# A hybrid decoder block on one core: shift columns by matmul, scaling on another engine, HGRN keys and states in other steps, first maxima under more matmuls

## The chip, the cores and the metric

The kernel runs on one core of a Trainium2 chip. The metric is the device time of one execution, in microseconds (us); the figure given for a kernel is the median of its runs. TensorE (PE in the profile, PEld for its weight loads) multiplies and writes to PSUM, VectorE (DVE) and ScalarE (ACT) read and write SBUF and PSUM, GpSimd (POOL) works on SBUF alone, and SyncE (SP) issues most DMAs. Each engine works through its own queue in order and waits at the head of it for whatever the next instruction needs.

## The reference, cut to what matters

The block has 2048 positions of width 1024. Everything is float32.

```python
mod = c_act @ w_ada + b_ada                       # shift, scale, gate, twice
h = rms_norm(x, norm1_g) * (1 + scale1) + shift1
hq, hf, hi, hgt, aq, ak, av = split(h @ w_in)
hg = hgrn2(hq, hf, hi, hgt)       # gated linear recurrence, 4 heads of 128, chunkwise
att = dilated_attention(aq, ak, av)  # 8 heads of 64, three (window, dilation) branches
x = x + gate1 * (concat(hg, rms_norm(att)) @ w_out)
h = rms_norm(x, norm2_g) * (1 + scale2) + shift2
x = x + gate2 * ((silu(h @ Wg) * (h @ Wu)) @ w_down)
out = rms_norm(x, final_g)
```

In the recurrence the state of a chunk is the decayed state before it plus keys times values, and a position's output is the query against the state before its chunk plus the scores inside the chunk times the values.

## The kernel before, in words

A float32 product is made of three fast matmuls: both operands are split into a high part and the rest (hi and lo), and hi·hi, hi·lo and lo·hi are added up in PSUM. A 512-wide matmul of this kind is called a **big** one below.

**Front.** `c_act` is known early. For each of the 8 blocks k of 128 features, `ada_sums` loads two 128x1024 blocks of `w_ada` (shift and scale; tile `adaw`, four buffers), DVE multiplies and adds them by k (two chains of 128x256 in `adaacc`, L105 and L107), and PE adds over the partitions with four matmuls against a column of ones (L110). A matmul with one output column is called a **small** one. ACT makes the shift (`mods`, L496) and scale (`gs1`, L497). `h_apply` then makes block k of the modulated input of the first chunk of 512 positions: times `rstd_x`, scaled and shifted on ACT (L416), split into `hhi` (ACT, L417) and `hlo`. The first and last of these steps run on POOL for chunk 0 and on DVE for the others. `token_major_k` (L463 to L465) multiplies block k with the weights of the values, twelve big matmuls a block. POOL also makes the low parts of the weights (`wlo`, in `split_w`). PE's order is written out by hand: small matmuls of block k, then the twelve big ones of block k-1.

**The two halves.** `first_half` and `second_half` run the input projection for two chunks each: `hg_project` and `att_qk` by `feature_major` (L565 to L567), `token_major` for the values. After every third big matmul `tick` runs the class `Beside`, which puts one step of other work between the matmuls when enough of them have passed: `begin(work, matmuls, steps)` spreads the steps over that many matmuls. The work is `hg_mix`, a generator that yields between steps. There are 16 units of it (4 heads, 4 chunks), two to a `begin`, and 33 steps are reckoned for the two. A unit makes gates and decays, transposes the decayed keys `kd` on PE (L620) to `kt` (copied by ACT, L622), makes `u` = keys times values (L657) and from it the states `hst` (DVE, L664 and L666), then the scores of seven levels (L677): PE writes a level's scores to the PSUM tile `psL`, DVE copies them under a mask into `hsc` (L680 or L682), and `level` prepares the products `hz` of the level two further on (POOL `hd`, ACT exp L644, DVE `hz`). The output `psO` (L693, L694) takes the states and `hsc`, and is normalised.

PSUM has eight banks here: four `psA` for the projections, two `psM`, one `psL`, one `psO`.

**The passage to attention.** After `second_half` the pool of the recurrence is closed, `open_attention` loads queries and keys of head 0, and `maxima(0)` runs its 24 steps between the last 96 big matmuls (`att_qk(1, 3)`), the first of them after 36. Then `combine(0)` joins the maxima of the three branches through DRAM (`m_d`, `mr`, `mn_d`), and the heads follow one after another; the maxima of head 1 (tile `psS`) come first there. SP issues all of these loads and the stores of `att_qk` from one queue.

The order of DVE, ACT, POOL and SP is made by a scheduler when the kernel is built; that of PE in these stages is that of the program.

Of the kernel before, what the change touches and what calls it, by code (L numbers as in the profile page):

```python
# [11 lines left out]
F32 = mybir.dt.float32  # L12
# [4 lines left out]
ALU = mybir.AluOpType  # L17
# [3 lines left out]
P = 128  # L21
# [9 lines left out]
CH = 512  # L31
NCH = S // CH
# [18 lines left out]
def hybrid_block(ctx, tc, xT, small, cst, w_ada, w_ft, w_tk, w_out, w_gu, w_dn, out):  # L51
# [27 lines left out]
    def tt(eng, o, a, b, op):  # L79
        return eng.tensor_tensor(o, a, b, op)  # L80
# [12 lines left out]
        act.activation(dst, dst, AF.Exp, scale=-0.5)  # L93


    def ada_sums(pl, cact, gs, bufs, psum, chains=1):

        w = pl.tile([P, 2, 8, P], F32, name="adaw", tag="adaw", bufs=bufs)
        acc = [pl.tile([P, 2, P], F32, name="adaacc", tag="adaacc", bufs=2 * chains) for _ in range(chains)]
        for j, g in enumerate(gs):  # L100
            nc.sync.dma_start(out=w[:, j].rearrange("p k c -> p (k c)"), in_=w_ada[g])
        for k in range(8):
            a = acc[k % chains]
            if k < chains:
                dve.tensor_scalar(a, w[:, :, k, :], cact[:, k:k + 1], None, ALU.mult)  # L105
            else:
                dve.scalar_tensor_tensor(a, w[:, :, k, :], cact[:, k:k + 1], a, ALU.mult, ALU.add)  # L107
        ps = psum()
        for j, a in [(j, a) for j in range(2) for a in range(chains)]:
            pe.matmul(ps[:, j:j + 1], acc[a][:, j, :], ones[:, 0:1], start=j + a == 0, stop=j + a == chains,  # L110
                      skip_group_check=True)
        return ps

    m_d = [[dram.tile([S], F32, name=f"m_d{h}_{n}") for n in range(2)] for h in range(8)]
# [223 lines left out]
    with ExitStack() as ab:  # L338
# [70 lines left out]

        def h_apply(c, k, t=None):  # L410
            hhi, hlo = h_of[c]
            eng = pool if c == 0 else dve
            if t is None:
                t = xs1[k] if c == 1 else load_xk(c, k)
            tt(eng, t, t, rstd_x[c], ALU.mult)
            act.activation(t, t, AF.Identity, scale=gs1[:, k:k + 1], bias=sh1[:, k:k + 1])  # L416
            act.copy(hhi[:, k, :], t)  # L417
            return tt(eng, hlo[:, k, :], t, hhi[:, k, :].bitcast(F32), ALU.subtract).ins

        def make_h(c):  # L420
            if c > 1:
# [46 lines left out]
        with tc.tile_pool(name="ada0", bufs=2) as pl:  # L468
            xs0 = []
            for k in range(KT):  # L470
                xs0.append(pl.tile([P, CH], F32, name=f"x0_{k}", bufs=1))
                nc.sync.dma_start(out=xs0[k], in_=xT[:, k, 0:CH])
            x_stats(0, xs0)
            h_tiles(0)
            ps0 = [pp.tile([P, CH], F32, name="psA", tag="psA", bufs=4) for _ in range(4)]
            tags = itertools.cycle(("psM", "psL"))

            def psum():
                tag = next(tags)
                return pp.tile([P, CH], F32, name=tag, tag=tag, bufs=2 if tag == "psM" else 1)  # L480

            LAG0 = 1

            bg = pl.tile([P, 8], F32, name="bg", bufs=1)
            dve.scalar_tensor_tensor(bg, sm[:, V_B + 8:V_B + 16], 1.0, sm[:, V_G1:V_G1 + 8], ALU.add, ALU.mult)
            sums, ws0 = {}, {}
            with tc.manual_schedule(engines={mybir.EngineType.PE}):
              done = {}
              for k in range(KT + LAG0):
                  if k < KT:  # L490
                      sums[k] = ada_sums(pl, cact, (k, 8 + k), 4, psum, 2)
                      if k % 2 == 0:
                          ws0[k] = ws0[k + 1] = split_w(wp, w_tk[0, k // 2])
                  if 0 < k <= KT:
                      n = k - 1
                      act.activation(mods[:, n:k], sums[n][:, 0:1], AF.Identity, bias=sm[:, V_B + n:V_B + k])  # L496
                      act.activation(gs1[:, n:k], sums[n][:, 1:2], AF.Identity, scale=sm[:, V_G1 + n:V_G1 + k],  # L497
                                     bias=bg[:, n:k])
                      with tc.issue_after(done[n - 2]) if n > 1 else nullcontext():
                          done[n] = h_apply(0, n, xs0[n])  # L500
# [92 lines left out]
        def hg_mix(hd, c, x):  # L593
# [21 lines left out]
            yield  # L615
            yield
            yield
            kt_ps = pp.tile([P, CH], F32, name="psM", tag="psM", bufs=2)
            for n in range(4):
                pe.transpose(kt_ps[:, n * P:(n + 1) * P], kd[:, n * P:(n + 1) * P], ident)  # L620
            kt = T("hkt")
            act.copy(kt, kt_ps)  # L622

            sc = T("hsc")
            lr = T("hd", 2)
# [20 lines left out]
                tt(dve, w(z)[:, :, 1, :], w(dd)[:, :, 1, :], w(q)[:, :, 1, :], ALU.mult)  # L646

            level(1)
            yield

            v = v_of[c]
            vn = [v[:, n, hd * P:(hd + 1) * P] for n in range(4)]
            ns = range(3 if c == NCH - 1 else 4)
            u = pp.tile([P, CH], F32, name="psM", tag="psM", bufs=2)
            for n in ns:
                ts = slice(n * P, (n + 1) * P)
                pe.matmul(u[:, ts], kt[:, ts], vn[n], start=n == 0, stop=n == ns[-1], skip_group_check=True)  # L657
            before = [states[hd]]
            for n in ns:
                ts = slice(n * P, (n + 1) * P)  # L660
                new = hw.tile([P, P], F32, name="hst", tag=f"hst{hd}", bufs=2) if n == 3 else \
                    hw.tile([P, P], F32, name="hst", tag="hst", bufs=3)
                if before[-1] is None:
                    dve.tensor_copy(new, u[:, ts])  # L664
                else:
                    dve.scalar_tensor_tensor(new, before[-1], eb[:, n * P + 127:n * P + 128], u[:, ts],  # L666
                                             ALU.mult, ALU.add)
                before.append(new)
            if len(ns) == 4:
                states[hd] = before[4]  # L670
# [40 lines left out]
        def units(hd, xs):  # L711
            return [hg_mix(hd, c, x) for c, x in xs.items()]
# [54 lines left out]

        first_psum = []

        def first_maxima():  # L770

            tags = itertools.cycle(("psL", "psO", "psM", "psM"))

            def psum():
                tag = next(tags)
                return pp.tile([P, CH], F32, name=tag, tag=tag, bufs=2 if tag == "psM" else 1)
            first_psum.append(psum)
# [631 lines left out]
```

## Time and profile before

| | us |
|---|---|
| time, median of 3 runs (lowest, highest) | 3009.27 (3007.25, 3016.14) |
| time of the profiled execution | 3006.01 |
| its span, first to last instruction | 3004.2 |
| PE busy | 2829.4 (94%) |
| DVE, ACT, POOL busy | 2041.7, 1313.2, 1404.8 |
| front, until the last product of chunk 0 | 0 to 68.9 |
| first and second half with the recurrence | 68.9 to about 908 |
| passage to attention | about 908 to 964 |

A row of the timeline gives start, busy time, engine, line, operation, tiles written and read, and a count; in brackets stands the idle time of the engine just ahead of it and what ended it. PE's matmuls overlap, so that the step from one start to the next is what a matmul takes. Mean granted clock of TensorE: 0.979 of full speed.

### The profile page before, as it was taken

What the parts mean: (1) busy time and instruction counts of PE and PEld (TensorE: products, weight loads), DVE (VectorE), ACT (ScalarE), POOL (GpSimd) and SP (SyncE); (2) the same over time, 40 slices, a digit from 0 to 9 for tenths busy, and PEclk for the clock granted to TensorE, in tenths of its full rate; (3) what the DMA queues carried; (4) which work ended last, traced back from release to release, by engine and by line L of the source; (5) the groups of instructions that cost most, each with busy time, mean ns of one, the idle gap of its engine ahead of it and who ended that gap; (6) DMA issues with size and microseconds to landing.
All of it is one profiled execution on the core that took longest, in us unless ns stands there. A gap on an engine that the chain in (4) does not pass through costs nothing. (4 is left out here: it accounts for less than half of the span.)

```text
span 3004.2 us, 45023 instructions
## 1 busy us (share of the span) xinstructions
PE 2829.4 (94%) x16308; PEld 2601.9 (87%) x16308; DVE 2041.7 (68%) x3781; ACT 1313.2 (44%) x2392; POOL 1404.8 (47%) x1076
## 2 busy tenths in 40 slices
PE   6899999999997999999999999999999998999998
PEld 4777777787776999997778999999999998999998
DVE  7677756355554565677777676688677669776676
ACT  4533445344331665666554333345333335443334
POOL 5333443434332232320045666557566655665664
PEclk9999999999997999999999999999999999999999
DMA  6422335111138474537843222123242222232221
GB/s 245 151 99 103 111 141 180 62 64 69 55 116 210 120 164 104 134 109 251 294 158 130 82 73 85 64 78 108 83 133 74 81 71 93 85 114 65 84 75 66
DMA packets 212319, 344.37 MB, mean 115 GB/s; under 512 B 24816, under 2 KB 97392, under 8 KB 209008
## 3 DMA queue, kind: packets, MB, share of 16 engines
q1 hardware_dynamic: 202272, 323.40, 34.9%
q10 hardware_dynamic: 9824, 18.09, 1.6%
q8 instruction: 128, 2.10, 0.3%
q14 instruction: 95, 0.78, 0.1%
HBM read 282.44 MB, written 58.98 MB: 114 GB/s over the span
## 5 line engine op out<-in xcount | busy, mean ns | idle before, releaser
L80 POOL TENSOR_TENSOR wlo<-wraw,whi 128x512 fp32r<-128x512 f32 (+1 forms) x542 | 850.0, 1589 | 480.5 <-ACT whi L87 222.1
L1003 PE MATMUL psG<-chi,whi 128*128 128x344 f32 (+1 forms) x1848 | 596.4, 323 | 20.8 <-DVE hm L80 14.1
L1005 PE MATMUL psG<-chi,wlo 128*128 128x344 f32 (+1 forms) x1848 | 591.9, 320 | 1.5 <-POOL wlo L80 1.5
L1004 PE MATMUL psG<-clo,whi 128*128 128x344 f32 (+1 forms) x1848 | 593.2, 321 | 0.0
L274 ACT CAST whi<-wraw 128x512 fp32r<-128x512 f32 x520 | 311.0, 618 | 403.9 <-issue 191.6
L1003 PEld LDWEIGHTS psG<-chi,whi 128*128 128x128 f32 x1848 | 350.3, 190 | 26.5 <-DVE hm L80 9.3
L1265 PE MATMUL psD<-ahi,whi 128*128 128x344 f32 (+1 forms) x1056 | 346.5, 328 | 20.2 <-DVE xc L1268 19.7
L1268 DVE SCALAR_TENSOR_TENSOR xc<-psD,mods,xc 128x344 f32<-128x344 f32 (+1 forms) x528 | 290.2, 568 | 91.8 <-PE psD L1267 91.5
L1005 PEld LDWEIGHTS psG<-chi,wlo 128*128 128x128 f32 x1848 | 349.3, 189 | 2.7 <-POOL wlo L80 2.7
L1004 PEld LDWEIGHTS psG<-clo,whi 128*128 128x128 f32 x1848 | 349.1, 189 | 0.3 <-issue 0.2
L80 POOL TENSOR_TENSOR wlo<-wt,whi 128x512 fp32r<-128x512 f32 x132 | 192.6, 1469 | 314.6 <-ACT whi L274 238.3
L1267 PE MATMUL psD<-ahi,wlo 128*128 128x344 f32 (+1 forms) x1056 | 338.0, 320 | 0.0
L1266 PE MATMUL psD<-alo,whi 128*128 128x344 f32 (+1 forms) x1056 | 337.0, 319 | 0.0
L80 DVE TENSOR_TENSOR hm<-hm,psG 128x344 f32<-128x344 f32 (+1 forms) x330 | 165.8, 502 | 236.9 <-PE psG L1005 236.5
L565 PE MATMUL psA<-hhi,whi 128*128 128x512 f32 x640 | 272.1, 425 | 4.3 <-ACT hhi L417 2.6
L567 PE MATMUL psA<-hhi,wlo 128*128 128x512 f32 x640 | 253.9, 397 | 0.0
L566 PE MATMUL psA<-hlo,whi 128*128 128x512 f32 x640 | 253.0, 395 | 0.6 <-DVE hlo L80 0.6
L1265 PEld LDWEIGHTS psD<-ahi,whi 128*128 128x128 f32 x1056 | 199.4, 189 | 36.1 <-DVE xc L1268 31.7
L80 POOL TENSOR_TENSOR hd<-hb 128x256 f32<-128x256 f32 x192 | 130.7, 704 | 155.4 <-DVE hz L80 123.3
L1266 PEld LDWEIGHTS psD<-alo,whi 128*128 128x128 f32 x1056 | 199.6, 189 | 0.5
L1267 PEld LDWEIGHTS psD<-ahi,wlo 128*128 128x128 f32 x1056 | 199.5, 189 | 0.0
L274 ACT CAST whi<-wt 128x512 fp32r<-128x512 f32 x132 | 81.4, 616 | 235.0 <-DVE wt L80 139.4
(244 smaller groups left out, 5996.6 us busy)
## 6 DMA issues: line engine op xcount, KB each, us to landing
wraw<-in_w_gu SPq DMA_DIRECT2D x264, 256.0 KB, 2.9
wraw<-in_w_dn SPq DMA_DIRECT2D x132, 256.0 KB, 2.9
adaw<-in_w_ada SPq DMA_DIRECT2D x48, 512.0 KB, 4.8
wraw<-in_w_ft SPq DMA_DIRECT2D x42, 512.0 KB, 3.5
wraw<-in_w_tk SPq DMA_DIRECT2D x32, 512.0 KB, 3.5
qk_d<-st SPq DMA_DIRECT2D x64, 256.0 KB, 2.3
v<-v_d SPq DMA_DIRECT2D x16, 1024.0 KB, 6.1
wraw<-in_w_out SPq DMA_DIRECT2D x64, 256.0 KB, 3.6
```

The lines of the kernel that those rows point to most:

```text
L80: return eng.tensor_tensor(o, a, b, op)
L274: copy(hi, raw)
L565: pe.matmul(ps, whi[:, ws], hhi[:, k, :], start=k == 0, stop=False)
L566: pe.matmul(ps, whi[:, ws], hlo[:, k, :], start=False, stop=False)
L567: pe.matmul(ps, wlo[:, ws], hhi[:, k, :], start=False, stop=k == 7)
L1003: pe.matmul(ps, w[0][:, ws], hi, start=start and k == 0, stop=False, skip_group_check=True)
L1004: pe.matmul(ps, w[0][:, ws], lo, start=False, stop=False, skip_group_check=True)
L1005: last = pe.matmul(ps, w[1][:, ws], hi, start=False, stop=stop and k == 3, skip_group_check=True)
L1265: pe.matmul(ps, w[z][0][:, ws], ahi, start=z == 0, stop=False)
L1266: pe.matmul(ps, w[z][0][:, ws], alo, start=False, stop=False)
L1267: pe.matmul(ps, w[z][1][:, ws], ahi, start=False, stop=z == 1)
L1268: dve.scalar_tensor_tensor(x, ps, ga2[:, j:j + 1], x, ALU.mult, ALU.add)
```

## The change

Four things are changed.

- `ada_sums` becomes `ada_column`. The shift column of block k is now made by eight small matmuls straight from the weights, and only the scale column goes through DVE's chains, which are 128 instead of 256 wide; two small matmuls add them up. `psL` has two buffers here as `psM` has.
- `h_apply` runs its two POOL steps on DVE for chunk 0 too, and no longer waits for the block before the last.
- In `hg_mix` the transposes of the keys (`turn`) come behind the first level's scores and the state updates behind the third level's, each in a step of its own (15 yields where there were 14). `psL` has two banks, and the output `psO` takes one of the two in turn; the bank of its own is gone.
- 48 big matmuls (`att_qk(1, 2)` on the last chunk) go from the last `begin` of the recurrence, whose 33 steps are now spread over 144 and not 192, behind `first_maxima`. The maxima are spread over 62 matmuls, the first after 50 and no longer 36, and `combine(0)` is a step of the same list, so that it stands between the big matmuls.

```diff
-    def ada_sums(pl, cact, gs, bufs, psum, chains=1):
+    def ada_column(pl, cact, k, bufs, psum):
...
+        acc = [pl.tile([P, P], F32, name="adaacc", tag="adaacc", bufs=4) for _ in range(2)]
+        for j, g in ((1, 8 + k), (0, k)):
...
+                dve.scalar_tensor_tensor(a, w[:, 1, k, :], cact[:, k:k + 1], a, ALU.mult, ALU.add)
         ps = psum()
-        for j, a in [(j, a) for j in range(2) for a in range(chains)]:
-            pe.matmul(ps[:, j:j + 1], acc[a][:, j, :], ones[:, 0:1], start=j + a == 0, stop=j + a == chains,
+        for k in range(8):
+            pe.matmul(ps[:, 0:1], w[:, 0, k, :], cact[:, k:k + 1], start=k == 0, stop=False, skip_group_check=True)
+        for a in range(2):
+            pe.matmul(ps[:, 1:2], acc[a], ones[:, 0:1], start=False, stop=a == 1, skip_group_check=True)
...
-            eng = pool if c == 0 else dve
...
-            kt_ps = pp.tile([P, CH], F32, name="psM", tag="psM", bufs=2)
...
             for lv in range(7):
+                if lv == 1:
+                    yield
+                    kt = turn()
+                elif lv == 3:
+                    yield
+                    before = state_updates(kt)
                 yield
                 zk, zq = zs.pop(lv)
-                ps = pp.tile([P, CH], F32, name="psL", tag="psL", bufs=1)
+                ps = pp.tile([P, CH], F32, name="psL", tag="psL", bufs=2)
...
-            o_ps = pp.tile([P, CH], F32, name="psO", tag="psO", bufs=1)
+            o_ps = pp.tile([P, CH], F32, name="psO", tag="psL", bufs=2)
...
-            beside.begin(units(3, xs), 192, 2 * UNIT + 1)
+            beside.begin(units(3, xs), 144, 2 * UNIT + 1)
             att_qk(1, 1)
-            att_qk(1, 2)
+            att_qk(1, 2, (2,))
...
-            beside.begin([maxima(0, psum)], 96 - 36, 24, -36)
+            beside.begin([maxima(0, psum), iter((combine(0, psum) for _ in range(1)))], 62, 24, -50)
...
+            att_qk(1, 2, (3,))
             att_qk(1, 3)
             beside.finish()
-        combine(0, first_psum[0])
```

How the order of the engines moves, at three places. The first is PE at the start, from the sum over squares (`ssq`) on. Before:

```order
L402 MATMUL psM<-ssq,ones 128x512
L110 MATMUL psM<-ones,adaacc 128x1 x4
L110 MATMUL psL<-ones,adaacc 128x1 x4
L463 MATMUL psA<-whi,hhi 128x512
L464 MATMUL psA<-wlo,hhi 128x512
L465 MATMUL psA<-whi,hlo 128x512
```

And in the changed kernel:

```order
L404 MATMUL psM<-ssq,ones 128x512
L111 MATMUL psM<-cact,adaw 128x1 x8
L113 MATMUL psM<-ones,adaacc 128x1 x2
L111 MATMUL psL<-cact,adaw 128x1 x8
L113 MATMUL psL<-ones,adaacc 128x1 x2
L464 MATMUL psA<-whi,hhi 128x512
L465 MATMUL psA<-wlo,hhi 128x512
L466 MATMUL psA<-whi,hlo 128x512
```

Ten small matmuls stand in a block's place where four stood, eight of them reading the weights as they were loaded.

The second place is ACT in the third unit of the recurrence, around the copy of the turned keys (`hkt`). `he` are the exponentials of a unit's gates, 128x1536, and `hd` at L644 (L638 in the changed kernel) the decays of a level. Before:

```order
L598 ACTIVATE he<-he 128x1536
L644 ACTIVATE hd<-hd 128x512 x2
L519 CAST st<-psA 128x512
L87 CAST whi<-wraw 128x1024
L644 ACTIVATE hd<-hd 128x512
L599 ACTIVATE he<-he 128x1536
L606 ACTIVATE hlf<-hfv 128x512
L622 COPY hkt<-psM 128x512
```

And in the changed kernel:

```order
L598 ACTIVATE he<-he 128x1536
L638 ACTIVATE hd<-hd 128x512 x2
L605 ACTIVATE hlf<-hfv 128x512
L638 ACTIVATE hd<-hd 128x512
L651 COPY hkt<-psM 128x512
L638 ACTIVATE hd<-hd 128x512
L87 CAST whi<-wraw 128x1024
```

The copy comes one level further on, behind `hlf` and one more `hd`. On PE 9 big matmuls stood between the transposes and `u` in this unit; now 21 big ones and the scores of two levels do.

The third place is SP at the end of the maxima of head 0: `qk_d<-st` are stores of `att_qk`, `m_d` and `mr` the maxima on their way, `kh` a load for head 1. Before:

```order
L575 DMA qk_d_0_86<-st 128x512
L150 DMA m_d_1_130<-mc 128x16
L153 DMA mr<-m_d_0_129 16x128
L576 DMA qk_d_1_87<-st 128x512
L213 DMA kh<-qk_d_0_80 64x2048
L153 DMA mr<-m_d_1_130 16x128
```

And in the changed kernel:

```order
L155 DMA mr<-m_d_0_129 16x128
L152 DMA m_d_1_130<-mc 128x16
L215 DMA kh<-qk_d_0_80 64x2048
L155 DMA mr<-m_d_1_130 16x128
L574 DMA qk_d_0_78<-st 128x512
L575 DMA qk_d_1_79<-st 128x512
```

The last four stores of `att_qk` come behind the load of `kh` and no longer ahead of it. On PE 30 big matmuls follow the last maxima of head 0, where none did; ahead of the first maxima stand 57 behind the last unit's sum of squares, where 54 stood.

## Rows read from the trace of the kernel before

**Rows 1.** Groups (--lines), 15 to 66 us, on DVE and POOL: busy, mean ns, idle.

```profile
L107 DVE SCALAR_TENSOR_TENSOR adaacc<-adaw,cact,adaacc 128x256 f32<-128x256 f32 x48 | 35.1, 796 | 0.0
L105 DVE TENSOR_SCALAR adaacc<-adaw,cact 128x256 f32<-128x256 f32 x16 | 9.6, 640 | 4.3 <-PE psM L110 1.9 <-DMA adaw<-in_w_ada 1.6 <-PE psL L110 0.9
...
L80 POOL TENSOR_TENSOR hlo<-x,hhi 128x512 fp32r<-128x512 f32 x8 | 14.7, 1833 | 11.2 <-ACT hhi L417 11.2
L80 POOL TENSOR_TENSOR wlo<-wraw,whi 128x1024 fp32r<-128x1024 f32 x5 | 12.5, 2496 | 0.0
L80 POOL TENSOR_TENSOR x<-x,rstd 128x512 f32<-128x512 f32 x8 | 11.0, 1377 | 16.7 <-ACT rstd L93 16.7
```

**Rows 2.** Timeline, DVE in the front, two runs of instructions with POOL idle.

```profile
27.30 2.45 DVE L107 SCALAR_TENSOR_TENSOR adaacc<-adaw,cact,adaacc 128x256 f32<-128x256 f32 x6
...
85.92 1.28 DVE L80 TENSOR_TENSOR hlo<-hx,hhi 128x512 fp32r<-128x512 f32 x2
```

**Rows 3.** Timeline, PE from the start to the end of chunk 0.

```profile
14.18 2.04 PE L402 MATMUL psM<-ssq,ones 128*128 128x512 f32 x2 [14.18 <-DVE ssq L80]
...
29.66 0.63 PE L463 MATMUL psA<-whi,hhi 128*128 128x512 f32 x1
...
30.09 0.63 PE L464 MATMUL psA<-wlo,hhi 128*128 128x512 f32 x1
...
52.83 0.48 PE L463 MATMUL psA<-whi,hhi 128*128 128x512 f32 x1
...
55.66 0.95 PE L110 MATMUL psM<-ones,adaacc 128*128 128x1 f32 x8
...
56.47 0.48 PE L463 MATMUL psA<-whi,hhi 128*128 128x512 f32 x1
...
68.90 0.39 PE L565 MATMUL psA<-hhi,whi 128*128 128x512 f32 x1
```

**Rows 4.** Waits of PE, 130 to 905 us: total, times, longest.

```profile
PE psL L677 <- DVE hsc L682: 23.1, 20, 2.2
PE psM L657 <- ACT hkt L622: 18.8, 10, 3.6
...
PE psM L620 <- DVE hkd L80: 2.3, 1, 2.3
PE psM L620 <- issue: 1.8, 1, 1.8
```

**Rows 5.** Timeline around one wait for the turned keys, ACT and PE.

```profile
187.55 1.48 ACT L599 ACTIVATE he<-he 128x1536 f32<-128x1536 f32 x1
188.94 0.57 ACT L622 COPY hkt<-psM 128x512 f32<-128x512 f32 x1
...
189.56 1.16 PE L657 MATMUL psM<-vtok,hkt 128*128 128x128 f32 x8 [2.49 <-ACT hkt L622]
```

**Rows 6.** Timeline around one wait for the scores' bank, DVE and PE.

```profile
203.25 0.70 DVE L682 COPY_PREDICATED hsc<-cs,psL 128x512 f32<-128x512 uint32 x1
...
204.00 1.16 PE L677 MATMUL psL<-hz 128*128 128x128 f32 x8 [0.97 <-DVE hsc L682]
```

**Rows 7.** Stretches: length, busy PE, PEld, DVE, ACT, POOL, granted clock, DMA.

```profile
130.00:905.00 775.00, 721.36 (x3723) 598.17 (x3722) 479.05 (x809) 309.05 (x421) 321.51 (x288) 0.98 0.29 100
...
160.00:180.00 20.00, 20.00 (x105) 17.00 (x105) 14.42 (x30) 5.09 (x8) 4.69 (x4) 0.91 0.23 79
...
800.00:820.00 20.00, 17.78 (x96) 15.08 (x95) 13.01 (x18) 4.52 (x6) 8.16 (x7) 0.91 0.16 53
```

**Rows 8.** Timeline in the passage to attention, PE, and one load on SP.

```profile
916.14 0.77 PE L133 MATMUL psL<-kh,qs 128*128 128x128 f32 x2 [8.13 <-DMA kh<-qk_d]
...
941.14 0.60 PE L896 MATMUL psT<-qs,kh 128*128 128x256 f32 x3
...
942.34 0.46 SPq L213 DMA_DIRECT2D kh<-qk_d  x1
...
947.91 1.62 PE L133 MATMUL psS<-kh,qs 128*128 128x128 f32 x6 [6.18 <-DMA mr<-m_d]
```

More of the change, by code (lines that the diff above doesn't have):

```diff
@@ L93, in rstd_of @@
         act.activation(dst, dst, AF.Exp, scale=-0.5)
-    def ada_sums(pl, cact, gs, bufs, psum, chains=1):
+    def ada_column(pl, cact, k, bufs, psum):
         w = pl.tile([P, 2, 8, P], F32, name="adaw", tag="adaw", bufs=bufs)
-        acc = [pl.tile([P, 2, P], F32, name="adaacc", tag="adaacc", bufs=2 * chains) for _ in range(chains)]
-        for j, g in enumerate(gs):
+        acc = [pl.tile([P, P], F32, name="adaacc", tag="adaacc", bufs=4) for _ in range(2)]
+        for j, g in ((1, 8 + k), (0, k)):
             nc.sync.dma_start(out=w[:, j].rearrange("p k c -> p (k c)"), in_=w_ada[g])
         for k in range(8):
-            a = acc[k % chains]
-            if k < chains:
-                dve.tensor_scalar(a, w[:, :, k, :], cact[:, k:k + 1], None, ALU.mult)
+            a = acc[k % 2]
+            if k < 2:
+                dve.tensor_scalar(a, w[:, 1, k, :], cact[:, k:k + 1], None, ALU.mult)
             else:
-                dve.scalar_tensor_tensor(a, w[:, :, k, :], cact[:, k:k + 1], a, ALU.mult, ALU.add)
+                dve.scalar_tensor_tensor(a, w[:, 1, k, :], cact[:, k:k + 1], a, ALU.mult, ALU.add)
         ps = psum()
-        for j, a in [(j, a) for j in range(2) for a in range(chains)]:
-            pe.matmul(ps[:, j:j + 1], acc[a][:, j, :], ones[:, 0:1], start=j + a == 0, stop=j + a == chains,
-                      skip_group_check=True)
+        for k in range(8):
+            pe.matmul(ps[:, 0:1], w[:, 0, k, :], cact[:, k:k + 1], start=k == 0, stop=False, skip_group_check=True)
+        for a in range(2):
+            pe.matmul(ps[:, 1:2], acc[a], ones[:, 0:1], start=False, stop=a == 1, skip_group_check=True)
         return ps
@@ L411, in h_apply @@
             hhi, hlo = h_of[c]
-            eng = pool if c == 0 else dve
             if t is None:
                 t = xs1[k] if c == 1 else load_xk(c, k)
-            tt(eng, t, t, rstd_x[c], ALU.mult)
+            tt(dve, t, t, rstd_x[c], ALU.mult)
             act.activation(t, t, AF.Identity, scale=gs1[:, k:k + 1], bias=sh1[:, k:k + 1])
             act.copy(hhi[:, k, :], t)
-            return tt(eng, hlo[:, k, :], t, hhi[:, k, :].bitcast(F32), ALU.subtract).ins
+            return tt(dve, hlo[:, k, :], t, hhi[:, k, :].bitcast(F32), ALU.subtract).ins
         def make_h(c):
@@ L479, in psum @@
                 tag = next(tags)
-                return pp.tile([P, CH], F32, name=tag, tag=tag, bufs=2 if tag == "psM" else 1)
+                return pp.tile([P, CH], F32, name=tag, tag=tag, bufs=2)
             LAG0 = 1
@@ L487, in hybrid_block @@
             with tc.manual_schedule(engines={mybir.EngineType.PE}):
-              done = {}
               for k in range(KT + LAG0):
                   if k < KT:
-                      sums[k] = ada_sums(pl, cact, (k, 8 + k), 4, psum, 2)
+                      sums[k] = ada_column(pl, cact, k, 4, psum)
                       if k % 2 == 0:
@@ L498, in hybrid_block @@
                                      bias=bg[:, n:k])
-                      with tc.issue_after(done[n - 2]) if n > 1 else nullcontext():
-                          done[n] = h_apply(0, n, xs0[n])
+                      h_apply(0, n, xs0[n])
                   if k >= LAG0:
@@ L617, in hg_mix @@
             yield
-            kt_ps = pp.tile([P, CH], F32, name="psM", tag="psM", bufs=2)
[L619 to L622, printed above, removed]
             sc = T("hsc")
@@ L648, in hg_mix @@
             level(1)
-            yield
             v = v_of[c]
             vn = [v[:, n, hd * P:(hd + 1) * P] for n in range(4)]
[L653 to L668, printed above, removed]
@@ L669, in hg_mix, with turn, state_updates @@
-            if len(ns) == 4:
-                states[hd] = before[4]
-            for lv in range(7):
+            def turn():
+                kt_ps = pp.tile([P, CH], F32, name="psM", tag="psM", bufs=2)
+                for n in range(4):
+                    pe.transpose(kt_ps[:, n * P:(n + 1) * P], kd[:, n * P:(n + 1) * P], ident)
+                kt = T("hkt")
+                act.copy(kt, kt_ps)
+                return kt
+            def state_updates(kt):
+                ns = range(3 if c == NCH - 1 else 4)
+                u = pp.tile([P, CH], F32, name="psM", tag="psM", bufs=2)
+                for n in ns:
+                    ts = slice(n * P, (n + 1) * P)
+                    pe.matmul(u[:, ts], kt[:, ts], vn[n], start=n == 0, stop=n == ns[-1], skip_group_check=True)
+                before = [states[hd]]
+                for n in ns:
+                    ts = slice(n * P, (n + 1) * P)
+                    new = hw.tile([P, P], F32, name="hst", tag=f"hst{hd}", bufs=2) if n == 3 else \
+                        hw.tile([P, P], F32, name="hst", tag="hst", bufs=3)
+                    if before[-1] is None:
+                        dve.tensor_copy(new, u[:, ts])
+                    else:
+                        dve.scalar_tensor_tensor(new, before[-1], eb[:, n * P + 127:n * P + 128], u[:, ts],
+                                                 ALU.mult, ALU.add)
+                    before.append(new)
+                if len(ns) == 4:
+                    states[hd] = before[4]
+                return before
```

6 lines of the change are left out of this document (2 added, 4 removed).

## The prediction

> **What bounds the kernel now.** I read the shares of the engines first (PE 2829.4 us busy of 3004.2, DVE as the next one 2041.7), then PE's waits by stretch, then the timeline at the longest of them. PE is the engine to shorten: an idle microsecond of PE is one of the kernel, unless another wait stands right behind it. There are three places. In the front, until 68.9 us [rows 3], PE waits for the first chunk, and this chunk for DVE and POOL, which hinder each other: six of DVE's 256-wide steps take 2.45 us (0.41 each) while POOL rests [rows 2], yet the mean of all 48 is 0.80 us [rows 1]; and POOL's 512-wide steps have a mean of 1.83 and 1.38 us. DVE and POOL are busy there for 44.7 and 38.2 us of 51. In the two halves PE waits 46.0 us in three kinds of wait that this change touches: 23.1 for the scores' bank, 18.8 for the turned keys, 4.1 at the transposes [rows 4]. In the passage to attention it waits 8.1 us for the first loads and 6.2 us before head 1 [rows 8].
>
> **Front.** Removed: half of DVE's columns and 16 POOL steps. Added: 16 steps of 512 on DVE and six small matmuls a block. DVE: a 512-wide step takes 0.62 us and a 256-wide one 0.41 [rows 2], so a line through both gives 0.31 for a 128-wide one; the two first ones of a chain are no dearer than that. A block then costs 8 x 0.31 + 2 x 0.62 = 3.7 us, eight cost 30. POOL keeps four `wlo` of 2.5 us [rows 1]; if each blocks DVE fully, that is 40 us, from about 15 to 55. PE: a small matmul is eight in 0.81 us for four of the program's (55.66 to 56.47), so 0.20 each at full rate; ten are 2.0. Twelve big ones are 2.83 us (52.83 to 55.66). Eight blocks make 8 x 4.83 = 38.7 us, and PE can begin when the first sum is out, at 16.2 [rows 3]: 54.9 if all of it ran at full rate. It does not. The big ones at 29.66 and 30.09 are 0.43 us apart, the 1.2 GHz level, though the clock is 2.4 GHz later. If the clock rises soon after 16.2, a stretch of 5 us loses 2.4; if only behind the first twelve big ones, two columns and these (3.8 + 3.8 + 5.1 = 12.7 us at the half rate) lose 6.4. Two of the `wlo` come late, since their casts stand on ACT behind a block's scaling: 0.5 us each. So chunk 0 ends between 58.3 and 62.3; I take 62, near what the big ones did before, and a gain of 7 us. PE, not DVE, is then last: DVE's 55 is the cover, and if POOL held it for longer, PE would wait for `hlo`. `adaw` buffers are now freed by PE too, but the eighth pair of loads is wanted only at about 50 us, so SP's queue is not last. What comes behind (statistics of chunk 1, its loads) hangs on the end of chunk 0, so I carry the 7 us on whole.
>
> On the clock, *TensorE: Matmul & The Clock Gate* of the Trainium skill (section "What's actually happening") states that the array is throttled by default and that recent activity of PE releases it; it does not say whether a one-column matmul, whose time is the loading of weights, counts as activity. If it counts, the early end (58.3) holds and the front gains 10.6; if not, the front can stay at the half rate. Both are rivals below.
>
> **Recurrence.** No matmul is added; the steps move. *Turned keys:* in the example the copy `hkt` stands on ACT behind `he` of 1.48 us, and PE waits 2.49 us for it [rows 5]. Now two levels of scores and 21 big matmuls (4.8 us at 0.227, a twelfth of rows 3's twelve) stand between the transposes and `u`, more than the longest of the ten waits, 3.6 [rows 4]. The copy goes past one `hd` on ACT; that `hd` serves scores two steps later. *Bank:* PE waits because `hsc` has not read the only bank [rows 6]. With two, level n waits for the copy of level n-2, a step earlier; a step is six to nine big matmuls and a level's scores, about 2.5 us, and the longest of the 20 waits is 2.2. What is next late is the products `hz`; they stand on DVE behind the copy of the level two back, so they too have a step in hand. The output takes a bank in turn; the second level of the next unit, which needs it again, stands eight steps later. *Transposes:* they come a step and a half later; scores of the first level now meet the wait for the unit's start, with one step more in hand. The state updates on DVE stand between two copies: DVE waits there for `u`, with the copy of the fourth level behind it, which PE needs only two levels on. I count 80% of 46.0 as gone: 36.8 us. The bounds are 50% (23; DVE late on its own) and all.
>
> *Clock:* eight stretches of 20 us in the halves have a granted clock of 0.91 (the first and the last in rows 7; the rest of the halves is at 1.00 but for one at the beginning), that is 3.6 us at 1.2 GHz and 1.8 us lost each, 14.4 in all. Each follows a wait of two or more us of the three kinds. I take 60%: 8.6 us; bounds 0 and 14.4. The recurrence gives 45 us (23 to 60).
>
> *The squeezed last pair:* a step is 4.4 big matmuls and a level, 2.1 us and not 2.4. Behind the output only three big ones (0.7 us) cover ACT's square of 0.6 and the way there and back: 0.5 us a unit, 1 us, inside the bounds.
>
> **Passage.** The first loads still come late: 57 big matmuls ahead of the first maxima where 54 stood (0.7 us more cover), but one store, which waits for 24 of them, stands ahead of the loads on SP. I leave that wait at 8.1, give or take 1. The second: PE is idle 6.2 us to 947.91, until `kh` of head 1, issued at 942.34, is there (the row names `mr`, which is on the same queue; my reading). Now 30 big matmuls, 6.8 us, stand in that hole, and `kh` is issued ahead of the stores. `combine` issues the same loads and stores, earlier, and its DVE steps no longer stand behind head 1's maxima. Gain 6.2, some 0.3 for the clock: 6.5 us, from 3 (`kh` no earlier, some of the work not hidden) to 10 (no half rate behind it).
>
> **The sum.** 7 + 45.4 + 6.5 = 58.9. The profiled execution took 3006.0, so 2947.1; the median of the runs stands 3.3 above the profiled one, so 2950. The forecast's own range, with 4 to 11, 28 to 58 and 3 to 10: 2930 to 2974.
>
> **Rivals.**
> A. *The wait moves on.* PE no longer waits for the bank but for `hz` or the next evacuation on the same DVE queue: half the waits and their clock stretches come back, the recurrence gives 15. Time 2980. For it: DVE carries 60 to 75% of a stretch [rows 7], in order. Against it: the waits were single late copies, with work to spare behind them.
> B. *The front stays at the half rate.* A block costs 4.83 x 0.43/0.227 = 9.1 us, eight 73: chunk 0 ends at about 90, 21 later instead of 7 earlier. Time 2979. Against it: eight of the records at 55.66 did not bring the rate down.
> C. *DVE becomes the bound of the halves: slower.* DVE is busy for 479 us of 775 [rows 7]. Where POOL interferes, its steps took 0.80 instead of 0.41 us in the front [rows 1, 2]. When PE runs without pauses, more of DVE's work can fall on POOL's; if DVE's time grows by half, it passes PE's own 715 us, and from there on the halves take DVE's time. At 1.7 times it is 815, 40 us longer than now; with the front's and the passage's gain that is 3036. Against it: it needs nearly all of DVE's steps to meet POOL, which is busy for 322 of 775.
> D. *The clock rises at once.* The front ends at 58.3 and gains 10.6 instead of 7: 2946. By the rule of the Trainium skill named above it would, if small matmuls count as activity.
> That the change does not do what it says is ruled out by the order of the engines: the steps stand where the text puts them.
>
> **How the numbers follow.** Forecast 0.62, A 0.17, B 0.08, C 0.05, D 0.08. Predicted: 2950. The range reaches from the likeliest case's best with D (2925) over most of A and B (2985); C, the upper parts of A and B and a small rest below are left out, some 0.18. A measurement of this kernel can tell about 0.3% (9 us) from no change. Faster by more than that (under 3000): all of the forecast but a little, D, and most of A and B, 0.89; within 0.3%: what is left of A and B, 0.05; slower: C and a rest, 0.06.
>
> **What would show it.** Front: the first big matmul on other weights than chunk 0's (68.90 before) at 58 to 62; no POOL step there but `wlo`; small matmuls 0.2 us each. Recurrence: PE's waits for `hsc` and `hkt` together under 10 us of 42, three or fewer stretches at 0.91. Passage: first wait still 7 to 9, the second under 2, and maxima of head 1 following big matmuls. Wrong: if `hz` takes the place of `hsc` among PE's waits (A); if the front's matmuls stay 0.43 us apart (B); if DVE is over 90% busy in the halves (C).

## The result, and the profile after

| | us |
|---|---|
| changed kernel, median of 4 runs (lowest, highest) | 2977.03 (2974.55, 2982.31) |
| kernel before, beside it | 3009.11 |
| ratio, 95% interval | 0.9895 (0.9883 to 0.9908) |
| its profiled execution, span | 2982.31, 2980.5 |

The change is worth 31.6 us (28 to 35), a little over half of the 58.9 forecast; the time lies inside the range and near rival A's 2980, and 3 us above the forecast's own range of 2930 to 2974. Below, a gain is one minus the ratio, times 3009 us.

PE's waits in the halves of the changed kernel, in the columns of [rows 4] (the wait for `kh` is the first one of the passage):

```profile
PE psL L688 <- DVE hz L80: 22.2, 17, 3.3
PE psL L135 <- DMA kh<-qk_d: 10.8, 1, 10.8
PE psA L564 <- DVE st L80: 5.2, 2, 4.0
PE psA L464 <- DVE st L80: 4.3, 2, 3.4
```

The waits for the bank, for the turned keys and at the transposes, 46.0 us before, are gone to the last one. In their place PE waits 22.2 us for `hz`, for which the profile of before lists no wait in the halves, and longer for `st`, the evacuations of the projections. The stretches that answer to [rows 7], with the front first:

```profile
14.00:62.00 48.00, 45.11 (x209) 39.07 (x210) 30.64 (x79) 16.88 (x33) 9.44 (x3) 0.86 0.54 203
130.00:905.00 775.00, 729.21 (x3773) 612.22 (x3772) 502.87 (x851) 311.18 (x425) 332.20 (x294) 0.97 0.33 109
...
200.00:220.00 20.00, 17.06 (x81) 14.44 (x80) 12.63 (x27) 4.54 (x7) 5.00 (x5) 0.83 0.25 92
```

The 0.97 of the 775 us takes in the first wait of the passage, which comes before 905 us here; from 130 to 860 us the mean clock is 0.98 in both kernels. The sixth column of numbers behind the length shows 0.83 in 200 to 220: a double stretch at 1.2 GHz (6.8 us) behind a wait of 2.94 us. In the front (answering to [rows 3]):

```profile
26.40 1.02 PE L113 MATMUL psL<-ones,adaacc 128*128 128x1 f32 x4 [2.59 <-DVE adaacc L108]
27.28 0.77 PE L464 MATMUL psA<-whi,hhi 128*128 128x512 f32 x1
...
32.01 1.84 PE L111 MATMUL psM<-cact,adaw 128*128 128x1 f32 x16
33.71 0.58 PE L113 MATMUL psM<-ones,adaacc 128*128 128x1 f32 x4
34.16 0.48 PE L464 MATMUL psA<-whi,hhi 128*128 128x512 f32 x1
...
35.08 0.63 PE L464 MATMUL psA<-whi,hhi 128*128 128x512 f32 x1
35.50 0.63 PE L465 MATMUL psA<-wlo,hhi 128*128 128x512 f32 x1
...
38.58 1.84 PE L111 MATMUL psL<-cact,adaw 128*128 128x1 f32 x16
...
73.42 0.39 PE L564 MATMUL psA<-hhi,whi 128*128 128x512 f32 x1
```

Chunk 0 ends at 73.42 us, 4.5 later than before and not 7 earlier. A block takes 6.57 us (32.01 to 38.58): the ten small matmuls 2.15 (2.0 forecast), but the twelve big ones 4.42 instead of 2.83, since most of them are 0.43 us apart. This block and the next three go much alike; in the one behind them, from 60.46, all twelve are 0.23 apart. And in the passage (answering to [rows 8]):

```profile
892.87 0.77 PE L135 MATMUL psL<-kh,qs 128*128 128x128 f32 x2 [10.83 <-DMA kh<-qk_d]
...
926.18 0.97 PE L135 MATMUL psS<-kh,qs 128*128 128x128 f32 x6 [1.05 <-DVE st L80]
```

The first wait has grown from 8.13 to 10.83 us: the last of the four loads is issued 1.6 us before PE runs dry (880.44 against 882.04), where it was 3.0 (905.01 against 908.01); and from that issue to the first maxima it takes 12.4 us and not 11.1. The second has fallen from 6.18 to 1.05.

### The profile page after: what moved, and what is told of

Read it like the earlier page. It is cut to its first block, busy times and chain, and to the rows that moved or that the text cites. A ratio compares the mean times of both kernels' runs of the same rounds, so it can differ in the third digit from the quotient of the medians.

```text
span 2980.5 us, 45292 instructions
## 1 busy us (share of the span) xinstructions
PE 2838.5 (95%) x16404; PEld 2618.9 (88%) x16404; DVE 2051.2 (69%) x3797; ACT 1313.5 (44%) x2394; POOL 1388.9 (47%) x1062
```

## The parts alone and together

Each of the first four kernels is the kernel before with one part of the change.

**The front alone** (one bank for the scores stays).

```diff
-                      sums[k] = ada_sums(pl, cact, (k, 8 + k), 4, psum, 2)
+                      sums[k] = ada_column(pl, cact, k, 4, psum)
...
-            eng = pool if c == 0 else dve
```

> The kernel before with the front's part of the change alone (shift column by small matmuls, DVE chains 128 wide, chunk 0 scaled on DVE; the scores keep one bank). Theory: each run of ten small matmuls lets the clock of the tensor engine fall for about 3.4 us, so a block takes 6.6 us and not 4.8; chunk 0 ends at 73 us (68.9 before) and the whole gets 3 to 6 us slower. Rival: the late end in the changed kernel comes from something the other parts do to the queues ahead; alone the front ends at 62 and the whole gets 5 to 8 us faster.

**The moved steps alone.**

```diff
+                if lv == 1:
+                    yield
+                    kt = turn()
+                elif lv == 3:
+                    yield
+                    before = state_updates(kt)
```

> The kernel before with the moved steps alone: keys turned behind the first level, states behind the third; one bank for the scores as before. Theory: the waits for the turned keys (18.8 us) vanish, those for the bank stay at 20 to 25 us, and the state updates on DVE, which now stand between two copies of scores, add 5 to 10 us of waits for the bank or for hz; gain 8 to 14 us. Rival (the waits for hz in the changed kernel come from the second bank alone, the moves are harmless): gain 17 to 25 us, waits for the bank as before, no wait for hz.

**The two banks alone.**

```diff
-                ps = pp.tile([P, CH], F32, name="psL", tag="psL", bufs=1)
+                ps = pp.tile([P, CH], F32, name="psL", tag="psL", bufs=2)
...
-            o_ps = pp.tile([P, CH], F32, name="psO", tag="psO", bufs=1)
+            o_ps = pp.tile([P, CH], F32, name="psO", tag="psL", bufs=2)
```

> The kernel before with two banks for the scores alone, the output taking one of them in turn. Theory (the moved states cause the waits for hz): the waits for the bank (23.1 us) vanish with less than 8 us of waits for hz in their place, those for the keys stay at 17 to 20; gain 14 to 22 us. Rival (the way POOL, ACT, DVE to hz is next late by itself): waits for hz of 15 to 23 us stand in place of those for the bank; gain 0 to 8 us.

**The passage alone.**

```diff
-            beside.begin(units(3, xs), 192, 2 * UNIT + 1)
+            beside.begin(units(3, xs), 144, 2 * UNIT + 1)
...
-            beside.begin([maxima(0, psum)], 96 - 36, 24, -36)
+            beside.begin([maxima(0, psum), iter((combine(0, psum) for _ in range(1)))], 62, 24, -50)
```

> The kernel before with the passage's part alone (48 matmuls moved behind the first maxima, last pair over 144 matmuls, joining of the maxima as a step). Theory: the wait of 6.2 us before head 1 falls under 1.5 us, the first wait stays between 8 and 11 us, and the stretch from the last big matmul to the scores of head 0 loses its half rate: gain 5 to 9 us. Rival: the squeezed last pair gives most of it back in waits for hz or the bank; gain under 3 us.

Two more put parts together: banks and moves, and these with the passage (the changed kernel with the front of before).

```diff
-                      sums[k] = ada_column(pl, cact, k, 4, psum)
+                      sums[k] = ada_sums(pl, cact, (k, 8 + k), 4, psum, 2)
```

> The kernel before with two banks and moved steps, front and passage as before. Alone the banks gave 17 us and the moves nothing, since 43 us of waits for the single bank took the place of 23 and of the keys' 19. Theory (the parts only work together: without the second bank the moved state updates are paid in waits for the bank, with it most of them lie under the level in hand): gain 25 to 33 us, waits for hz 18 to 24 us, none for the keys. Rival (the moves give nothing with two banks either, and the rest of the whole change's 32 us comes from front and passage, which get cheaper beside the others): gain 15 to 20 us.

> The changed kernel with the front of before. Theory: the front is worth nothing or costs up to 5 us (chunk 0 ends at 73 us in the changed kernel, at 69 before), so this version takes 2971 to 2978 us. Rival (chunk 0's later end is paid back by what it hides behind it): 2980 to 2986 us.

| | median | ratio (95%) | gain, us |
|---|---|---|---|
| front alone | 3007.73 | 0.9997 (0.9988, 1.0007) | 0.9 |
| moves alone | 3007.27 | 0.9999 (0.9990, 1.0009) | 0.3 |
| banks alone | 2990.83 | 0.9942 (0.9927, 0.9957) | 17.5 |
| passage alone | 3010.72 | 1.0010 (1.0000, 1.0020) | -3.0 |
| banks and moves | 2980.71 | 0.9908 (0.9885, 0.9932) | 27.7 |
| banks, moves, passage | 2971.23 | 0.9878 (0.9863, 0.9892) | 36.7 |
| all four: the change | 2977.03 | 0.9895 (0.9883, 0.9908) | 31.6 |

Alone the four gains add up to 15.7 us, together they give 31.6. PE's waits in the halves show why. With the moves alone:

```profile
PE psL L689 <- DVE hsc L694: 39.9, 22, 3.7
...
PE psL L689 <- DVE hsc L80: 3.5, 4, 1.2
```

The keys' 18.8 us are gone, as forecast, but the bank's 23.1 have become 43.4: the stall has changed its name. Both theories of this run gave a gain, and there is none. With the banks alone:

```profile
PE psM L657 <- ACT hkt L622: 18.9, 10, 3.6
PE psL L677 <- DVE hz L80: 8.2, 9, 1.9
```

Here the bank's 23.1 us are replaced by only 8.2 for `hz`, while the keys' stay: the theory of that run holds, but for the 8.2, which it put under 8. With both, 18.8 us for `hz`:

```profile
PE psL L689 <- DVE hz L80: 18.8, 15, 3.0
```

So the second bank takes most of its waits away for good, and the moves put 10 to 20 us of new ones on DVE's queue, with either number of banks. That the moves are worth about 10 us beside the banks and nothing without them is the theory stated for the pair, and its forecast came true (25 to 33 us, 18 to 24 for `hz`, none for the keys); the interval of the pair (20 to 35 us) starts where its rival's 15 to 20 ends, and overlaps a little with that of the banks alone. 27.7 with 36.7 and 36.7 with 31.6 make the passage worth 9 us and the front -5, each give or take some 6 to 8 us, since the intervals are wide and near each other; the version with the front of before fell into the 2971 to 2978 that its theory gave. The front alone is within 3.6 us of nothing in time, less than the loss its theory told, though chunk 0 ends late there as it said. In the traces 5.4 us of it are still there at the last scores of the recurrence, which start at 894.1 us, 888.7 before; what gives some of them back behind that is not shown.

```profile
74.59 0.39 PE L564 MATMUL psA<-hhi,whi 128*128 128x512 f32 x1
```

The passage alone gains nothing, against its theory, though its first wait fell to 5.4 us. The rival does not explain it: in the last `begin` PE waits 5.2 us for keys and bank, where it waited 4.7 before. It shows a wait of its own. SP and PE there:

```profile
901.35 14.05 SPq L575 DMA_DIRECT2D qk_d<-st  x1
...
916.97 0.64 SPq L84 DMA_DIRECT2D wraw<-in_w_ft  x1
```

```profile
924.35 0.80 PE L565 MATMUL psA<-hhi,whi 128*128 128x512 f32 x1 [4.96 <-ACT whi L87]
```

The load of the weights for the last 48 matmuls stands behind a store that sits 14 us at the head of SP's queue, and PE waits 4.96 us for them, most of what the other two waits give. That the median is 3 us longer is not shown to come from it: the profiled execution is 4.1 us late at 705 us already, at a wait for the keys that ends at 709.55 and ended at 705.42 before, ahead of all that this part changes. In the changed kernel that load is issued at 873.24, before the first loads of head 0, and the wait is not there. The 6.2 us before head 1 are gone in both.

## Where the wait for `hz` comes from

DVE in the changed kernel, around the state updates of one unit, where PE waits 3.27 us for `hz` until 376.33:

```profile
370.66 1.23 DVE L606 TENSOR_TENSOR_SCAN hb<-rst,hlf 128x512 f32<-128x512 f32 x1 [0.51 <-POOL hd L80]
371.80 0.32 DVE L669 SCALAR_TENSOR_TENSOR hst<-hst,heb,psM 128x128 f32<-128x128 f32 x1
372.04 1.31 DVE L736 SCALAR_TENSOR_TENSOR adaacc<-adaw,cact,adaacc 128x256 f32<-128x256 f32 x1
...
374.58 0.33 DVE L669 SCALAR_TENSOR_TENSOR hst<-hst,heb,psM 128x128 f32<-128x128 f32 x1
374.84 0.71 DVE L693 COPY_PREDICATED hsc<-cs,psL 128x512 f32<-128x512 uint32 x1
375.45 0.41 DVE L80 TENSOR_TENSOR hz<-hd,hk 128x256 f32<-128x256 f32 x1
375.77 0.41 DVE L80 TENSOR_TENSOR hz<-hd,hq 128x256 f32<-128x256 f32 x1
```

```profile
376.33 0.98 PE L688 MATMUL psL<-hz 128*128 128x128 f32 x3 [3.27 <-DVE hz L80]
```

The scan `hb` already belongs to the next unit, and waits for POOL's `hd`, which reads that tile; behind it come four updates of the state (`hst`), with steps of the later `w_ada` sums (`adaacc`) between them, then the copy of the scores, and only then the `hz` for which PE waits. From the end of the scan to the copy it takes 3 us: 1.3 are the updates, the rest the steps between them. These steps are not needed for such a wait: at 169.30 and 209.50 PE waits 2.40 and 2.94 us behind a scan and updates with no `adaacc` among them. The next two kernels leave the scan where it is and move only the updates.

```diff
-                elif lv == 3:
+                elif lv == 5:
                     yield
                     before = state_updates(kt)
```

> The changed kernel with one move other: the states are updated behind the fifth level, not the third. In the changed kernel DVE's order has the next unit's scan hb (1.23 us, after a wait for POOL) and then the four state updates in one run, ahead of a copy of scores and the hz of that level; behind the fifth level no hz is left to make. Theory (that run of DVE work is what PE waits for): the waits for hz fall from 22 to under 10 us, and the whole gets 8 to 16 us faster than the changed kernel, to 2961 to 2969. Rival (hz is late by its own way over POOL and ACT): waits for hz stay at 17 to 23 us and the time within 4 us of the changed kernel's 2977.

```diff
-                elif lv == 3:
+                elif lv == 2:
                     yield
                     before = state_updates(kt)
```

> The changed kernel with the states updated behind the second level, not the third. The scan of the next unit then no longer stands directly ahead of the updates, but these still stand ahead of a copy of scores and of hz. Theory (scan and updates in one run are the trouble): the waits for hz fall to 8 to 16 us, the time to 2964 to 2973. Rival (any place of the updates ahead of hz costs the same): waits for hz of 17 to 23 us, time within 4 us of 2977.

Behind the fifth level: 2955.62 us, ratio 0.9826 (0.9806 to 0.9845), a gain of 52.4. The same place of the program, and PE's waits for `hz` in the halves:

```profile
361.39 1.23 DVE L606 TENSOR_TENSOR_SCAN hb<-rst,hlf 128x512 f32<-128x512 f32 x1 [0.52 <-POOL hd L80]
362.53 0.71 DVE L693 COPY_PREDICATED hsc<-cs,psL 128x512 f32<-128x512 uint32 x1
363.13 0.95 DVE L80 TENSOR_TENSOR hz<-hd,hk 128x256 f32<-128x256 f32 x1
```

```profile
PE psL L688 <- DVE hz L80: 9.2, 8, 2.6
```

The copy now follows the scan at once, and the waits for `hz` fall from 22.2 to 9.2 us. Behind the second level: 2970.77 us, 0.9874 (0.9859 to 0.9889), 6 us under the changed kernel, with intervals that overlap a little. Its waits:

```profile
PE psL L688 <- DVE hz L80: 17.1, 12, 2.4
```

So the place of the updates is the cause of the larger part of these waits, and the rival of the first of these runs (that `hz` is late by its own way over POOL and ACT) falls: that way is the same in all three. What is left behind the fifth level, 9.2 us, is near the 8.2 of the banks alone. The second run leaves its own question open: the time came out as the theory had it, the waits stayed in the 17 to 23 of its rival. What it costs that the updates stand right behind the scan, and not only ahead of an `hz`, is not shown apart.

## The front

Both kernels are the version with the states behind the fifth level and another front. The first keeps the scaling on DVE and makes the shift column by DVE's chains again:

```diff
-                      sums[k] = ada_column(pl, cact, k, 4, psum)
+                      sums[k] = ada_sums(pl, cact, (k, 8 + k), 4, psum, 2)
```

> The changed kernel with the states behind the fifth level (2955.6 us) and, in the front, only half of the change: chunk 0 is scaled on DVE, but the shift column comes from the 256-wide DVE chains again, with four small matmuls a block. Theory (the run of ten small matmuls is what lowers the clock and costs the front its gain, the scaling on DVE is good): DVE needs 8 x 0.41 + 2 x 0.62 = 4.5 us a block and is the bound, chunk 0 ends at 58 to 66 us instead of 73, and the time is 2942 to 2951 us. Rival (DVE alone is too slow without POOL's help): chunk 0 ends at 70 to 76, time 2953 to 2960.

The second has the column's small matmuls one by one between the big ones:

```diff
                 pe.matmul(ps[n], hhi[:, k, ts], whi[:, cs_], start=k == 0, stop=False)
+                if small:
+                    small.popleft()()
...
-            LAG0 = 1
+            LAG0 = 2
```

> The changed kernel with the states behind the fifth level (2955.6 us); in the front the ten small matmuls of a column stand one by one between the twelve big ones, two blocks behind, instead of ten in a row. The same matmuls, in another order. Theory (the row of small ones lowers the clock): with one small between big ones the clock stays at its upper level after the first block, a block takes 4.8 to 5.2 us, chunk 0 ends at 60 to 66 us and the time is 2943 to 2950. Rival (small matmuls lower the clock wherever they stand): six half-rate stretches as before, chunk 0 ends at 71 to 76 us, time 2953 to 2960.

With the scaling alone: 2947.06 us, 0.9805 (0.9789 to 0.9821), a gain of 58.7, as its theory had it. The interval overlaps a little with that of the front it replaces (0.9806 to 0.9845); in the traces chunk 0 ends 10.9 us earlier, at 62.25 and not 73.18, and 10.2 us of it are left at the end of the spans (2941.7 and 2951.9). DVE's chains, the same instructions as in [rows 1], take 474 ns on average in this kernel where they took 796:

```profile
62.25 0.39 PE L562 MATMUL psA<-hhi,whi 128*128 128x512 f32 x1
```

```profile
L107 DVE SCALAR_TENSOR_TENSOR adaacc<-adaw,cact,adaacc 128x256 f32<-128x256 f32 x48 | 19.6, 474 | 0.0
```

Without POOL's 16 steps on chunk 0 DVE's are that much shorter, by 0.32 us on each of 48 instructions. The Trainium skill (*SBUF — State Buffer*, section "Who interferes with whom") states that an instruction of DVE with two inputs from SBUF contends with one of GpSimd that reads SBUF; the trace agrees.

With the small ones spread, the forecast of the run was wrong in sign, and its rival, right on the clock, fell short in size: 2975.60 us, 0.9900 (0.9885 to 0.9915), 22 us worse than in a row. PE's matmuls, and two stretches with 27 to 86 last:

```profile
29.04 0.77 PE L470 MATMUL psA<-whi,hlo 128*128 128x512 f32 x1
29.62 0.42 PE L110 MATMUL psM<-cact,adaw 128*128 128x1 f32 x2
29.90 0.78 PE L464 MATMUL psA<-whi,hhi 128*128 128x512 f32 x1
...
83.38 0.63 PE L470 MATMUL psA<-whi,hlo 128*128 128x512 f32 x1
...
90.62 0.39 PE L573 MATMUL psA<-hhi,whi 128*128 128x512 f32 x1
```

```profile
14.00:62.00 48.00, 45.06 (x160) 39.79 (x161) 28.52 (x70) 13.72 (x25) 9.41 (x3) 1.00 0.54 206
27.00:86.00 59.00, 59.00 (x201) 51.61 (x201) 26.15 (x61) 16.84 (x32) 10.03 (x4) 1.00 0.30 109
```

PE is busy for 59.00 of 59.00 us, and a big and a small matmul together take 0.86 us (29.04 to 29.90) from 27 us to the end of the last column. That is the 1.2 GHz level: a big matmul behind small ones has 0.77 us in such a row, as at 27.28 in the changed kernel, and 0.48 at the full rate, as at 34.16 there. Only behind the last column, and seven more big ones 0.43 apart from 83.38 on, do they come to 0.23. So it is not the row of ten as such: in turn with the big ones the small matmuls went with the lower level all through, and in a row a part of the big ones ran at the upper one. (The kernel differs in the lag too, two blocks instead of one; PE has no wait in this stretch that this could explain.)

## The passage

Two kernels on the first wait. The first is the version with the states behind the fifth level, and hands over the loads that the maxima don't need later:

```diff
+            def first():
+                for i, _ in enumerate(maxima(0, psum)):
+                    if i == 5:
+                        prep_x(0, early["qk"])
+                        prep_v(0, 0, early["v"])
+                    yield
```

> The changed kernel with the states behind the fifth level (2955.6 us); in the passage the loads of head 0 that the maxima don't need (qx, kl, v; 2 MB) are issued six steps into the maxima instead of right behind those that they need (qs, kh). Theory (the first wait of 10.8 us is the loads sharing the DMA engines): the wait falls to 5 to 8 us and the half rate behind it gets shorter; time 2948 to 2953. Rival (the 2 MB that are needed take that long by themselves): the wait stays at 10 to 11 us, time 2953 to 2958.

It took 2956.17 us, 0.9835 (0.9819 to 0.9850), with a wait of 10.5 us. It settles nothing on the sharing: SP's order, which the scheduler makes, put these loads only a few microseconds later, still ahead of the first maxima at 874.29:

```profile
862.15 0.64 SPq L213 DMA_DIRECT2D kh<-qk_d  x1
866.57 0.45 SPq L219 DMA_DIRECT2D qx<-qk_d  x1
```

The second stands on the version with the scaling alone in the front:

```diff
-            beside.begin([maxima(0, psum), iter((combine(0, psum) for _ in range(1)))], 62, 24, -50)
+            beside.begin([maxima(0, psum), iter((combine(0, psum) for _ in range(1)))], 42, 24, -70)
```

> The version with the states behind the fifth level and only the scaling on DVE in the front (2947.1 us), and in the passage the maxima of head 0 begin after 70 big matmuls instead of 50 and are spread over 42 instead of 62; the same matmuls, in another order. DVE is busy for 16.5 of the 24.6 us of the maxima, so that they can stand closer. Theory (20 more big ones, 4.5 us at 0.227, cover the loads): the first wait falls from 10.6 to 6 or 7 us, nothing new behind it, time 2940 to 2944 us. Rival (the maxima become DVE's bound, or their end no longer comes before the loads and the joining for head 1): what the first wait gives comes back as waits for mc or before head 1; time 2945 to 2950.

```profile
PE psL L133 <- DMA kh<-qk_d: 6.2, 1, 6.2
PE psS L133 <- DVE mc L141: 1.3, 3, 0.6
PE psS L133 <- DVE st L80: 1.1, 1, 1.1
```

The wait falls from 10.6 to 6.2 us, as the 20 matmuls ahead of it make out, and nothing new stands behind it. The time is 2944.91 us, 0.9790 (0.9774 to 0.9806): the best of all, 63 us (58 to 68) under the kernel before. Over the version without this edit it is 2 us by the medians and 4.5 by the ratios; the intervals overlap, so that this last step is shown in the trace and not in the time.

## Why the prediction was right or wrong

- **The time** lies in the range, but in its upper half: 31.6 us of gain where 58.9 were added up. The range holds it because rivals A and B were drawn into it; the forecast's own ended at 2974. Of its signs of being wrong the first came true, and the second in part. Two terms failed.
- **Recurrence: 45.4 forecast, 27.7 measured** with banks and moves (20 to 35), just under its 28 to 58. The step that failed is the one on the state updates: "DVE waits there for `u`, with the copy of the fourth level behind it, which PE needs only two levels on". The copy is not what PE needs, the `hz` behind the copy is, and it needs that one soon. The step on the bank, "they too have a step in hand", left the updates and the scan out of the count; with the banks alone, the updates at their old place, `hz` was already late by 8.2 us. Of the 46.0 us of waits not 80% went but, with 22.2 come back as `hz`, 52%; the evacuations took some more.
- **Clock in the halves: +8.6 forecast.** It went the other way: eight stretches of 3.4 us at 1.2 GHz before, ten behind 130 us and ahead of the passage now. The waits have become fewer and longer: four of 2.9 us or more, where there was one, and behind three of these four (at 209.50, 477.00 and 500.44) stands a double stretch. The clock term was taken in proportion to the waits' number. That their length decides is not shown either: before, no stretch follows the longest wait (3.60 us, until 872.07), nor the one of 2.49 in [rows 5]. And the waits ahead of the eight stretches are of 1.87 to 2.31 us, not all of "two or more".
- **Rival A was the mechanism**, `hz` in the place of `hsc`, with 2980 for its time, and a chance of 0.17 only. What spoke against it ("single late copies, with work to spare behind them") was read off the kernel before, in which the updates stood elsewhere. Moved by one line, the updates give back most of what the forecast had promised: 52.4 us for the whole.
- **Front: +7 forecast, 0 to -5 measured.** DVE and POOL were sized well enough not to be the bound behind the first block: POOL has only `wlo` left, and DVE's four kinds of step take 34 us from 15 to 66 us, where 30 were reckoned (groups below; `hlo` has 1.18 us each and not 0.62, the first ones of a chain 0.58 and not 0.31). What failed is the term of 2.83 us for twelve big ones, and with it rival B's counter-argument, "eight of the records at 55.66 did not bring the rate down": behind twenty of them it fell. The block is 6.57 us and not 4.83, and 1.59 of these 1.74 us are in the twelve big ones. Of the 11.4 us by which chunk 0 ends later than 62, some 8 are of this kind; 2.59 are PE's wait for DVE's chain until 26.40, which the sum left out. Spread among them the small ones gave rival B's end of about 90 us (90.62). Rival D's early end did not come.

```profile
L108 DVE SCALAR_TENSOR_TENSOR adaacc<-adaw,cact,adaacc 128x128 f32<-128x128 f32 x47 | 13.0, 341 | 0.0
L80 DVE TENSOR_TENSOR hlo<-x,hhi 128x512 fp32r<-128x512 f32 x7 | 8.3, 1184 | 13.7 <-ACT hhi L418 13.7
L106 DVE TENSOR_SCALAR adaacc<-adaw,cact 128x128 f32<-128x128 f32 x14 | 7.5, 577 | 0.0
L80 DVE TENSOR_TENSOR x<-x,rstd 128x512 f32<-128x512 f32 x8 | 5.1, 680 | 5.1 <-ACT rstd L93 5.1
```

- **Passage: 6.5 forecast (3 to 10), 9 measured** beside banks and moves, give or take 8. The wait before head 1 went as told (1.05 us left). The first wait, told to stay at 7 to 9, is 10.8. That the part alone gains nothing, with a weight load caught behind a store on SP, was not foreseen; every DMA that the moved `att_qk` issues had to be counted, and its weights were not.
- **Rival C** did not come: DVE is busy for 503 of 775 us, 24 more than before, with more of the work in the same time.
- **A reading:** 0.227 us is not a twelfth of the 2.83 in [rows 3], which is 0.236; it is the step between two big ones that follow each other. No term hangs on it.

## What to carry to other kernels

When a wait on an engine's queue is taken away, or work is moved in it, follow that queue past the instruction that is freed to the next thing that the bound engine needs, and put the moved work where nothing behind it is wanted soon: one line (third or fifth level) was 21 us here. Try the parts of a change together as well as alone: three of the four were worth nothing by themselves, and the moved steps because the wait that they uncovered is one that the second bank removes. And count small matmuls at the price they put on the big ones around them.

## What the runs showed of the hardware

PE can work without a pause and stay at the lower of its two levels: from 27 us on, with one-column matmuls in turn with 512-wide ones, it was busy for 59.00 of 59.00 us, and a pair took 0.86 us, as at 1.2 GHz, until the small ones were through. *TensorE: Matmul & The Clock Gate* of the Trainium skill (section "What's actually happening") says that activity releases the throttle. The prediction's open question, whether small matmuls do, is answered by this run for this order: the rate did not rise as long as they stood between the big ones. And the granted clock stood at 1.00 in those rows, though the big ones took 0.57 us each to the next start, and 0.23 later: in the first stretch of an execution the distance between matmuls is to be read, and not that column.
